# A hybrid decoder layer on one core: memory attention of two samples at a time, and three PSUM tiles of the recurrence in other banks

## The chip, the cores and the metric

The kernel runs on one core of one Trainium2 chip. The metric is device time in microseconds (us) of one execution, as a median over runs. Engines: PE does matmuls (PEld its weight loads), DVE, ACT and POOL do elementwise work, SP issues the weight DMAs and POOL's own queue (GpSimd) the rest.

## The reference

One decoder layer on 256 prompt tokens and 64 sample tokens (8 samples of 8), all in fp32:

```
xn = RMSNorm(x); p = xn @ w_in            # RWKV r,k,v,decay,a,gate | SWA q,k,v | memory q | 3 gates
A: RWKV-7, 12 heads of 64:  S = S*w + (S@-kk)(kk*a) + v k;  o = S @ r      # a scan over tokens
   o = (groupnorm(o) + bonus) * (sigmoid(gl) @ w_gate_up)
B: sliding-window attention (128), 12 query and 4 key heads, learned sinks
C: cross attention, 4 heads of 128, into 256 memory tokens per sequence:
   s = q . mk * 128**-0.5;  o = softmax(s) @ mv     # prompt: computed mk, mv; sample b: its cache_mem_k/v
merged = sum_i sigmoid(gate_i) * (o_i @ w_br_i);  h = x + RMSNorm(merged @ w_o)
y = h + RMSNorm((gelu(conv3(z_gate)) * z_val) @ w_ffn_down)
```

The change touches branch A (the recurrence) and the sample half of branch C.

## The kernel before, in words

Every weight matrix is streamed once in blocks of 128 x 128. A weight chunk `raw` comes by SP's queue, ACT casts its high half `wh` (L374, L97) and DVE takes the low half `wl` (L375, L98); `mm3` (L101 to L104) then does three matmuls of 320 columns per block. These "big" matmuls make up most of the program, and all other work of PE is put in between them.

What puts it there is `pump` (L404): the recurrence and the attention are generators, "threads", that issue some instructions and yield a number, the modelled time until their next piece may stand; between pieces `step` (L378) issues one block of big matmuls and moves a modelled clock on by 0.405. The order of PE's instructions is therefore written out when the program is built, and kept. For DVE, ACT, POOL and SP a scheduler sets the order.

The recurrence (about 90 to 530 us) goes over six pairs of heads, hp0 to hp5, in chunks of 32 tokens: 8 of the prompt, 2 of the samples. Each pair has three generators.
- `early` (L509) builds the operands `ar`, `bk` on DVE and ACT; PE takes the scores of all chunks into two PSUM tiles, `ps1` and `ps2` (L566, L571, L572); DVE masks them into `BT` (L569), POOL sends them through DRAM (L579, L581) to `NI`.
- `inverse` (L633) inverts the triangles of the chunks on DVE (L643 to L663), a long chain of multiplies and reductions; its result goes by DRAM (L666, POOL) and back as `IT` (four DMAs of L671, POOL).
- `late` (L677) solves (L693), takes the samples' states in (L714; ACT copies the result to `Wu`, L716), forms the chunk steps (L724 on PE into two banks; DVE adds them into `AB`, L727, and into `ar`, L730), starts the state in `psb` (L734), turns the 64 sample rows `Wu` by four small matmuls with the identity (L739, tile `psu`), which DVE adds to `AU` (L743, one instruction for each head), and starts the output `pso` from `BT` and `AU` (L749, 16 matmuls). Then the chain over chunks runs, PE (L753) and ACT by turns, each step with a yield of 1.2 (HOP). Behind it come the sample states (L769, L771 to L773), the group norm (L780, L781, L783; `rstd` with L130, POOL's power L136 and the copy L139; L147, L789), and the gate (L793, tile `psg`) with L794 and L795.

PSUM in the recurrence has eight banks: `big` two, `pea` two and `pch` two (both hand out tiles named `sm`; `bank()` in `late` takes one of `pch`), `pso` one and `psb` one. A tile of `pea` or `pch` is handed out again when the readers of the tile before last are done.

In the attention (about 530 to 800 us) PSUM is `big`, four banks of `smp` and two accumulators. `mem_sample` (L931) goes over the 8 samples: keys `ck` and values `cv` by POOL's queue (L937, L939, two buffers each), four score matmuls (L944), softmax (L885), two transposes (L902) and a DVE copy (L905), and eight matmuls into `po` (L952). The rows of a group of 32 that do not belong to the sample have probability 0 by the mask `smask`, so that four samples sum up in one tile.

Of the kernel before, what the change touches and what calls it, by code (L numbers as in the profile page):

```python
# [9 lines left out]
F32 = mybir.dt.float32  # L10
# [6 lines left out]
T = 320  # L17
TP = 256
# [21 lines left out]
SOFT = 3.5  # L40
SSOFT2, TRN2 = 9.0, 3.6
TRN = 2.0
# [21 lines left out]
def tile_hybrid_step(ctx: ExitStack, tc: tile.TileContext, i, o):  # L64
    nc = tc.nc
    V, A, G, PE = nc.vector, nc.scalar, nc.gpsimd, nc.tensor
# [9 lines left out]
    C = {n: cst[:, s] for n, s in COFF.items()}  # L76
# [351 lines left out]
    with tc.tile_pool(name="rws", bufs=1, side="right") as rws, tc.tile_pool(name="rwp", bufs=2, side="right") as rwp, \  # L428
# [80 lines left out]
        def early(hp):  # L509
# [58 lines left out]
            def masked(pv, lo, hi, mask):  # L568
                V.tensor_mul(out=BT[:, lo:hi, 64:128], in0=pv, in1=C[mask].unsqueeze(1).to_broadcast([128, hi - lo, 64]))  # L569

            ps1 = pea.tile([128, 512], F32, tag="sm", name="sm").rearrange("p (c t) -> p c t", t=64)  # L571
            ps2 = pea.tile([128, 512], F32, tag="sm", name="sm").rearrange("p (c t) -> p c t", t=64)  # L572
            scores(ps1, 0, 8)
            scores(ps2, 8, 10)
            masked(ps1, 0, 8, "tmask")
# [101 lines left out]
        def late(hp, ar, pc, bonus, BT, it, AU, AP):  # L677
# [9 lines left out]
            def bank():  # L687
                return pch.tile([128, 512], F32, tag="sm", name="sm")
# [43 lines left out]
            for c in range(8):  # L732
                for h in range(2):
                    PE.matmul(psb[fss[h], 64 * c:64 * c + 64], BT[fss[h], c, 0:64], AU[fss[h], c, 64:128],  # L734
                              start=c == 0, stop=c == 7, skip_group_check=True)
            psu = bank()
            for cc in range(2):
                for h in range(2):
                    PE.matmul(psu[uss[h], 64 * cc:64 * cc + 64], Wu[fss[h], 32 * cc:32 * cc + 32], C["ident"][fss[h], fss[h]], start=True, stop=True)  # L739
            SA = rw1.tile([128, 8, 64], F32, tag="SA", name="SA")  # L740
            A.activation(out=SA[:, 0, :], in_=psb[:, 0:64], func=AF.Copy, scale=pc[:, 0:1])
            for h in range(2):
                V.tensor_add(out=AU[uss[h], 8:10, 64:128], in0=psu[uss[h], 0:128].rearrange("p (c v) -> p c v", v=64), in1=AU[uss[h], 8:10, 64:128])  # L743
            UVm = rw1.tile([128, 512], F32, tag="UVm", name="UVm").rearrange("p (c s v) -> p c s v", s=4, v=64)
            G.tensor_mul(out=UVm, in0=AU[:, 8:10, 64:128].unsqueeze(2).to_broadcast([128, 2, 4, 64]),
                         in1=C["smask"].unsqueeze(1).unsqueeze(3).to_broadcast([128, 2, 4, 64]))
# [42 lines left out]
            V.tensor_mul(out=ob, in0=ob, in1=rn)  # L789
            A.activation(out=ob, in_=ob, func=AF.Identity, scale=col("lnw", hp), bias=col("lnb", hp))  # L790
            yield 2.0
            psg = pea.tile([128, 512], F32, tag="sm", name="sm")[:, :T]
            PE.matmul(psg, lw[:, 1, cs], lora[1], start=True, stop=True)  # L793
            V.tensor_add(out=ob, in0=ob, in1=bonus)  # L794
            V.tensor_mul(out=ob, in0=psg, in1=ob)  # L795
# [51 lines left out]
    with tc.tile_pool(name="at", bufs=1, side="right") as at, tc.tile_pool(name="at2", bufs=2, side="right") as at2, \  # L847
# [37 lines left out]
        def softmax(src, n, scale, th, keep=None):  # L885
            mx = at2.tile([128, 1], F32, tag="mx" + th, name="mx")
            V.tensor_reduce(out=mx, in_=src, axis=AX.X, op=ALU.max)
            V.tensor_scalar(out=mx, in0=mx, scalar1=-scale, scalar2=None, op0=ALU.mult)
            pr = at2.tile([128, 384], F32, tag="pr" + th, name="pr")[:, :n]
            sm = at2.tile([128, 1], F32, tag="sum" + th, name="sum")  # L890
            A.activation(out=pr, in_=src, func=AF.Exp, scale=scale, bias=mx, accum_out=sm)
            V.reciprocal(out=sm, in_=sm)
            if keep is None:
                V.tensor_scalar(out=pr, in0=pr, scalar1=sm, scalar2=None, op0=ALU.mult)
            else:
                V.tensor_scalar(out=pr, in0=pr, scalar1=sm, scalar2=keep, op0=ALU.mult, op1=ALU.mult)
            return pr
# [31 lines left out]
            state["om"] += 1  # L929

        def mem_sample():  # L931
            for b in range(8):
                bg, s = b // 4, b % 4
                if s == 0:
                    po = accp.tile([128, 512], F32, tag="accs", name="psos")
                ck = at2.tile([128, 4, 256], F32, tag="ck", name="ck")
                nc.gpsimd.dma_start(out=ck, in_=i["cmk"][b])  # L937
                cv = at2.tile([128, 2, 512], F32, tag="cv", name="cv")
                nc.gpsimd.dma_start(out=cv, in_=i["cmv"][b])  # L939
                yield 4.0  # L940
                pss = smp.tile([128, 512], F32, tag="sm", name="sm")
                qc = TP + 32 * bg
                for h in range(4):
                    PE.matmul(pss[32 * h:32 * h + 32, 0:256], MQ[:, h, qc:qc + 32], ck[:, h, :], start=True, stop=True,  # L944
                              tile_position=(0, 32 * h))
                pr = softmax(pss[:, 0:256], 256, MS, "s", C["smask"][:, s:s + 1])
                yield SOFT
                pt = transposed(pr, ((0, 128), (128, 128)), "s")
                yield TRN
                for kb in range(2):  # L950
                    for h in range(4):
                        PE.matmul(po[32 * h:32 * h + 32, 0:128], pt[:, 128 * kb + 32 * h:128 * kb + 32 * h + 32],  # L952
                                  cv[:, kb, 128 * h:128 * h + 128], start=s + kb == 0, stop=s + kb == 4, tile_position=(0, 32 * h))
                if s == 3:
                    ob = at2.tile([128, 128], F32, tag="ob", name="ob")
                    A.copy(out=ob, in_=po[:, 0:128])
                    yield TRN
                    pst = smp.tile([128, 512], F32, tag="sm", name="sm")
                    PE.transpose(pst[:, 0:128], ob, C["ident"])
                    split(OMH[:, :, qc:qc + 32], OML[:, :, qc:qc + 32], pst[:, 0:128].rearrange("p (h t) -> p h t", t=32))  # L960
            state["om"] += 1
# [440 lines left out]
```

## Time and profile before

| | |
|---|---|
| median of 3 runs | 2039.72 us (2036.27 to 2040.2) |
| the profiled execution | 2036.6 us, its span 2034.8 |
| PE busy, of the span | 1981.6 us (97%) |
| DVE, ACT, POOL busy | 1215.6 (60%), 829.2 (41%), 195.7 (10%) |
| mean granted TensorE clock | 0.988 |

A busy share is an average over stages. The rows below are taken from three kinds of view: busy time in stretches of the span, the list of what an engine waited for, and the timeline, in which a row is one instruction or a run of like ones ("x32"; a matmul of fp32 data is counted twice, since it runs in two passes), and in brackets the idle time of that engine just ahead and what ended it.

### The profile page before, as it was taken

The page shows a single profiled execution, that of the slowest core. Times are in us where ns is not written, and L with a number is a line of the kernel's source. Part 1 is how long each engine was busy: PE and PEld are TensorE (multiplying, and loading weights), DVE is VectorE, ACT ScalarE, POOL GpSimd, SP SyncE. Part 2 cuts the span into 40 slices and gives each one's busy share as a digit, 9 for nine tenths or more (in the row PEclk, how much of TensorE's full clock was granted, in tenths as well). Part 3 has the DMA queues.
Part 4 walks back from the last instruction along what each step waited for, and adds up shares of the span by engine and source line. Part 5 has one row for each costly group of instructions (what it writes and reads, how often), then busy time and mean ns, then how long its engine had stood idle before and what let it go on. Part 6 is the DMA issues. An engine that isn't in the chain of part 4 may idle for free.

```text
span 2034.8 us, 36379 instructions
## 1 busy us (share of the span) xinstructions
PE 1981.6 (97%) x14888; PEld 1928.4 (95%) x14888; DVE 1215.6 (60%) x2019; ACT 829.2 (41%) x1353; POOL 195.7 (10%) x446
## 2 busy tenths in 40 slices
PE   8999898899999999999999999999999999999997
PEld 8888898889998999999999999999999999999997
DVE  7788868874467754444447653554555555555456
ACT  5544344333444433333444433333343333343335
POOL 4412122211200000000100100000000000000001
PEclk9999899999999999999999999999999999999999
DMA  7543343333645444544552444454444444444433
GB/s 277 174 140 120 95 134 102 101 103 128 203 169 160 136 130 153 160 152 150 194 187 91 155 145 153 148 179 161 150 151 147 154 146 155 146 155 146 151 135 127
DMA packets 89688, 303.28 MB, mean 149 GB/s; under 512 B 11500, under 2 KB 13190, under 8 KB 89504
## 3 DMA queue, kind: packets, MB, share of 16 engines
q1 hardware_dynamic: 79920, 273.42, 40.1%
q0 software_dynamic: 8880, 26.71, 3.9%
q8 instruction: 117, 1.92, 0.4%
q10 hardware_dynamic: 720, 0.82, 0.1%
q14 instruction: 51, 0.42, 0.1%
HBM read 293.53 MB, written 9.34 MB: 149 GB/s over the span
## 4 chain that ended last, share of the span: by engine, by line
PE 57%; issue 5%; POOL 1%; DVE 0%; ACT 0%; POOLq 0%; DVEq 0%
PE bigps L102 18%; PE bigps L103 18%; PE bigps L104 18%; PE bigps L1171 0%; PE bigps L1169 0%; PE bigps L1172 0%; POOL merged L1094 0%; POOL yacc L1259 0%; POOL yacc L1260 0%; DVE MG L845 0%; PE sm L147 0%; POOL rsr L1119 0%; PE sm L1244 0%; PE sm L1112 0%; PE sm L1247 0%
## 5 line engine op out<-in xcount | busy, mean ns | idle before, releaser
L102 PE MATMUL bigps<-XH,wh 128*128 128x320 f32 x2656 | 843.7, 318 | 0.9 <-ACT gt L862 0.8
L104 PE MATMUL bigps<-XH,wl 128*128 128x320 f32 x2656 | 824.0, 310 | 1.4 <-DVE wl L375 1.3
L103 PE MATMUL bigps<-XL,wh 128*128 128x320 f32 x2656 | 823.7, 310 | 0.0
L98 DVE TENSOR_TENSOR wl<-raw,wh 128x1024 fp32r<-128x1024 f32 (+1 forms) x299 | 357.5, 1195 | 275.3 <-ACT wh L97 274.7
L97 ACT CAST wh<-raw 128x1024 fp32r<-128x1024 f32 (+1 forms) x299 | 306.5, 1025 | 521.5 <-PE bigps L103 412.8
L102 PEld LDWEIGHTS bigps<-XH,wh 128*128 128x128 f32 x2656 | 501.6, 189 | 14.1 <-issue 8.6
L103 PEld LDWEIGHTS bigps<-XL,wh 128*128 128x128 f32 x2656 | 501.9, 189 | 2.2 <-issue 0.2
L104 PEld LDWEIGHTS bigps<-XH,wl 128*128 128x128 f32 x2656 | 501.3, 189 | 2.4 <-DVE wl L375 2.4
L375 DVE TENSOR_TENSOR wl<-raw,wh 128x1024 fp32r<-128x1024 f32 (+2 forms) x212 | 243.2, 1151 | 184.5 <-ACT wh L374 182.0
L374 ACT CAST wh<-raw 128x1024 fp32r<-128x1024 f32 (+2 forms) x212 | 208.4, 984 | 313.0 <-PE bigps L103 250.9
L103 PE MATMUL bigps<-fl,wh 128*128 128x320 f32 x704 | 217.5, 309 | 0.0
L102 PE MATMUL bigps<-fh,wh 128*128 128x320 f32 x704 | 217.4, 309 | 0.0
L104 PE MATMUL bigps<-fh,wl 128*128 128x320 f32 x704 | 217.4, 309 | 0.0
L102 PEld LDWEIGHTS bigps<-fh,wh 128*128 128x128 f32 x704 | 132.2, 188 | 0.2 <-ACT fh L152 0.2
L103 PEld LDWEIGHTS bigps<-fl,wh 128*128 128x128 f32 x704 | 132.2, 188 | 0.1
L104 PEld LDWEIGHTS bigps<-fh,wl 128*128 128x128 f32 x704 | 132.2, 188 | 0.0
L1228 DVE TENSOR_TENSOR yacc<-yacc,bigps 128x320 f32<-128x320 f32 x80 | 38.9, 487 | 84.4 <-PE bigps L104 84.4
L1202 POOL COPY cout<-zp 128x9 f32<-128x9 f32 x88 | 15.5, 206 | 734.0 <-DVE zp L1199 734.0
L102 PE MATMUL bigps<-MG,wh 128*128 128x320 f32 x208 | 64.4, 309 | 0.3 <-ACT MG L844 0.3
L103 PE MATMUL bigps<-MG,wh 128*128 128x320 f32 x208 | 64.3, 309 | 0.0
L104 PE MATMUL bigps<-MG,wl 128*128 128x320 f32 x208 | 64.3, 309 | 0.0
L1198 DVE TENSOR_TENSOR zp<-bigps,S 128x256 f32<-128x256 f32 x44 | 18.7, 425 | 57.0 <-PE bigps L104 57.0
(407 smaller groups left out, 2358.4 us busy)
## 6 DMA issues: line engine op xcount, KB each, us to landing
raw<-in_wup SPq DMA_DIRECT2D x176, 512.0 KB, 3.5
raw<-in_win SPq DMA_DIRECT2D x164, 512.0 KB, 3.6
raw<-in_wdn SPq DMA_DIRECT2D x80, 512.0 KB, 3.2
raw<-in_wo SPq DMA_DIRECT2D x32, 512.0 KB, 3.7
raw<-in_wbr_rw SPq DMA_DIRECT2D x16, 384.0 KB, 3.2
raw<-in_wbr_sw SPq DMA_DIRECT2D x16, 384.0 KB, 3.1
ck<-in_cmk POOLq DMA_DIRECT2D x8, 512.0 KB, 5.1
cv<-in_cmv POOLq DMA_DIRECT2D x8, 512.0 KB, 4.2
```

What stands on the lines that cost most here:

```text
L97: A.copy(out=h, in_=raw)
L98: V.tensor_sub(out=l, in0=raw, in1=h.bitcast(F32))
L102: PE.matmul(ps, h, xh, start=start, stop=False)
L103: PE.matmul(ps, h, xl, start=False, stop=False)
L104: PE.matmul(ps, l, xh, start=False, stop=stop)
L374: A.copy(out=h, in_=c[2])
L375: V.tensor_sub(out=l, in0=c[2], in1=h.bitcast(F32))
L1198: V.tensor_mul(out=zp[:, 2:258], in0=psz[:, 0:TP], in1=S2[:, 0:TP])
L1202: G.tensor_copy(out=cout[:, j, :, e], in_=zp[:, 256 + e:337 + e:10])
L1228: V.tensor_add(out=yacc[:, m, :], in0=yacc[:, m, :], in1=ps)
```

## The change

1. The two score tiles of `early` come from `pch` instead of `pea`.
2. The gate's tile `psg` comes from `bank()`, so from `pch`, instead of `pea`.
3. `psu` is no bank of its own any more: it is columns 384 to 511 of the tile `pso`, which hold nothing else (the output has 0 to 255, the samples' rows 256 to 383). Its matmuls do not start the accumulation anew (`start=False`).
4. `mem_sample` takes two samples at a time: four DMAs ahead, eight score matmuls into one bank, two softmaxes, four transposes and one copy of 512 columns, sixteen matmuls; its yields are 5.0, 9.0 (SSOFT2) and 3.6 (TRN2) in place of 4.0, 3.5 (SOFT) and 2.0 (TRN).

```diff
--- before.py
+++ after.py
@@ -568,8 +568,8 @@
             def masked(pv, lo, hi, mask):
                 V.tensor_mul(out=BT[:, lo:hi, 64:128], in0=pv, in1=C[mask].unsqueeze(1).to_broadcast([128, hi - lo, 64]))
 
-            ps1 = pea.tile([128, 512], F32, tag="sm", name="sm").rearrange("p (c t) -> p c t", t=64)
-            ps2 = pea.tile([128, 512], F32, tag="sm", name="sm").rearrange("p (c t) -> p c t", t=64)
+            ps1 = pch.tile([128, 512], F32, tag="sm", name="sm").rearrange("p (c t) -> p c t", t=64)
+            ps2 = pch.tile([128, 512], F32, tag="sm", name="sm").rearrange("p (c t) -> p c t", t=64)
             scores(ps1, 0, 8)
             scores(ps2, 8, 10)
             masked(ps1, 0, 8, "tmask")
@@ -733,14 +733,15 @@
                 for h in range(2):
                     PE.matmul(psb[fss[h], 64 * c:64 * c + 64], BT[fss[h], c, 0:64], AU[fss[h], c, 64:128],
                               start=c == 0, stop=c == 7, skip_group_check=True)
-            psu = bank()
+            psu = pso[:, TP + 128:TP + 256]
             for cc in range(2):
                 for h in range(2):
-                    PE.matmul(psu[uss[h], 64 * cc:64 * cc + 64], Wu[fss[h], 32 * cc:32 * cc + 32], C["ident"][fss[h], fss[h]], start=True, stop=True)
+                    PE.matmul(psu[uss[h], 64 * cc:64 * cc + 64], Wu[fss[h], 32 * cc:32 * cc + 32], C["ident"][fss[h], fss[h]],
+                              start=False, stop=True, skip_group_check=True)
             SA = rw1.tile([128, 8, 64], F32, tag="SA", name="SA")
             A.activation(out=SA[:, 0, :], in_=psb[:, 0:64], func=AF.Copy, scale=pc[:, 0:1])
             for h in range(2):
-                V.tensor_add(out=AU[uss[h], 8:10, 64:128], in0=psu[uss[h], 0:128].rearrange("p (c v) -> p c v", v=64), in1=AU[uss[h], 8:10, 64:128])
+                V.tensor_add(out=AU[uss[h], 8:10, 64:128], in0=psu[uss[h], :].rearrange("p (c v) -> p c v", v=64), in1=AU[uss[h], 8:10, 64:128])
             UVm = rw1.tile([128, 512], F32, tag="UVm", name="UVm").rearrange("p (c s v) -> p c s v", s=4, v=64)
             G.tensor_mul(out=UVm, in0=AU[:, 8:10, 64:128].unsqueeze(2).to_broadcast([128, 2, 4, 64]),
                          in1=C["smask"].unsqueeze(1).unsqueeze(3).to_broadcast([128, 2, 4, 64]))
@@ -789,7 +790,7 @@
             V.tensor_mul(out=ob, in0=ob, in1=rn)
             A.activation(out=ob, in_=ob, func=AF.Identity, scale=col("lnw", hp), bias=col("lnb", hp))
             yield 2.0
-            psg = pea.tile([128, 512], F32, tag="sm", name="sm")[:, :T]
+            psg = bank()[:, :T]
             PE.matmul(psg, lw[:, 1, cs], lora[1], start=True, stop=True)
             V.tensor_add(out=ob, in0=ob, in1=bonus)
             V.tensor_mul(out=ob, in0=psg, in1=ob)
@@ -929,29 +930,40 @@
             state["om"] += 1
 
         def mem_sample():
-            for b in range(8):
-                bg, s = b // 4, b % 4
-                if s == 0:
+            for b2 in range(4):
+                bg, s0 = b2 // 2, 2 * (b2 % 2)
+                if s0 == 0:
                     po = accp.tile([128, 512], F32, tag="accs", name="psos")
-                ck = at2.tile([128, 4, 256], F32, tag="ck", name="ck")
-                nc.gpsimd.dma_start(out=ck, in_=i["cmk"][b])
-                cv = at2.tile([128, 2, 512], F32, tag="cv", name="cv")
-                nc.gpsimd.dma_start(out=cv, in_=i["cmv"][b])
-                yield 4.0
+                kv = []
+                for s in range(2):
+                    ck = at2.tile([128, 4, 256], F32, tag="ck", name="ck")
+                    nc.gpsimd.dma_start(out=ck, in_=i["cmk"][2 * b2 + s])
+                    cv = at2.tile([128, 2, 512], F32, tag="cv", name="cv")
+                    nc.gpsimd.dma_start(out=cv, in_=i["cmv"][2 * b2 + s])
+                    kv.append((ck, cv))
+                yield 5.0
                 pss = smp.tile([128, 512], F32, tag="sm", name="sm")
                 qc = TP + 32 * bg
                 for h in range(4):
-                    PE.matmul(pss[32 * h:32 * h + 32, 0:256], MQ[:, h, qc:qc + 32], ck[:, h, :], start=True, stop=True,
-                              tile_position=(0, 32 * h))
-                pr = softmax(pss[:, 0:256], 256, MS, "s", C["smask"][:, s:s + 1])
-                yield SOFT
-                pt = transposed(pr, ((0, 128), (128, 128)), "s")
-                yield TRN
-                for kb in range(2):
-                    for h in range(4):
-                        PE.matmul(po[32 * h:32 * h + 32, 0:128], pt[:, 128 * kb + 32 * h:128 * kb + 32 * h + 32],
-                                  cv[:, kb, 128 * h:128 * h + 128], start=s + kb == 0, stop=s + kb == 4, tile_position=(0, 32 * h))
-                if s == 3:
+                    for s in range(2):
+                        PE.matmul(pss[32 * h:32 * h + 32, 256 * s:256 * s + 256], MQ[:, h, qc:qc + 32], kv[s][0][:, h, :],
+                                  start=True, stop=True, tile_position=(0, 32 * h))
+                prs = [softmax(pss[:, 256 * s:256 * s + 256], 256, MS, "s", C["smask"][:, s0 + s:s0 + s + 1]) for s in range(2)]
+                yield SSOFT2
+                pst = smp.tile([128, 512], F32, tag="sm", name="sm")
+                for s in range(2):
+                    for kb in range(2):
+                        PE.transpose(pst[:, 256 * s + 128 * kb:256 * s + 128 * kb + 128], prs[s][:, 128 * kb:128 * kb + 128], C["ident"])
+                pt = at2.tile([128, 512], F32, tag="pt2", name="pt2", bufs=1)
+                V.tensor_copy(out=pt, in_=pst)
+                yield TRN2
+                for s in range(2):
+                    for kb in range(2):
+                        for h in range(4):
+                            c0 = 256 * s + 128 * kb + 32 * h
+                            PE.matmul(po[32 * h:32 * h + 32, 0:128], pt[:, c0:c0 + 32], kv[s][1][:, kb, 128 * h:128 * h + 128],
+                                      start=s0 + s + kb == 0, stop=s0 + s + kb == 4, tile_position=(0, 32 * h))
+                if s0 == 2:
                     ob = at2.tile([128, 128], F32, tag="ob", name="ob")
                     A.copy(out=ob, in_=po[:, 0:128])
                     yield TRN
```

Line numbers behind the first edit of `late` go up by one in the changed kernel (L743 is L744, L749 is L750, L753 is L754, and so on), and in `mem_sample` the scores L944 are L949. Three places show how the order moves.

PE, the recurrence, `late` of hp0, before (with the engines that each instruction waits for):
```order
L724 MATMUL sm<-BT,AU 64x96 [waits DVE_49,PE_49,Activation_49]
L724 MATMUL sm<-BT,AU 64x96 [waits DVE_49]
L724 MATMUL sm<-BT,AU 64x96 x6
L724 MATMUL sm<-BT,AU 64x96 [waits PE_49]
L724 MATMUL sm<-BT,AU 64x96 x5
L734 MATMUL psb<-AU,BT 64x64 x16
L739 MATMUL sm<-cst,Wu 32x64 [waits DVE_49,PE_49,Activation_49]
L739 MATMUL sm<-cst,Wu 32x64 x3
L749 MATMUL pso<-BT,AU 64x32 x16
```
And after:
```order
L724 MATMUL sm<-BT,AU 64x96 [waits DVE_49,PE_49,Activation_49]
L724 MATMUL sm<-BT,AU 64x96 [waits DVE_49]
L724 MATMUL sm<-BT,AU 64x96 x6
L724 MATMUL sm<-BT,AU 64x96 [waits PE_49]
L724 MATMUL sm<-BT,AU 64x96 x5
L734 MATMUL psb<-AU,BT 64x64 x16
L739 MATMUL pso<-cst,Wu 32x64 [waits Activation_49]
L739 MATMUL pso<-cst,Wu 32x64 x3
L750 MATMUL pso<-BT,AU 64x32 [waits DVE_49]
```
The order of PE is the same; L739 writes `pso`, loses its waits for DVE and PE and keeps ACT's, and the first L750 has a wait for DVE that L749 did not have.

On DVE nothing moves at this step: in every pair the two adds stand behind L727, L727, L730, L727, L727, L730, and read `pso` now.

POOL, where the late part of hp0 meets the inverse of hp1, before:
```order
L772 TENSOR_TENSOR S_1389<-S_1389,pc 128x512 [waits DVE_49]
L773 DMA out_wkvs<-S_1389 128x512 [waits DMASW2_49,Pool_49]
L666 DMA sc_2523<-R 120x192 [waits DMASW3_49,DVE_49]
L474 COPY shout<-pad 128x9 [waits Activation_49]
L681 DMA S_2208<-in_wkv 128x512 [waits DMASW4_49,DMASW2_49]
L469 MEMSET pad 128x1 [waits DVE_49,Pool_49]
L470 COPY pad<-shs 128x8
L671 DMA IT_775<-sc_2523 32x5x32 [waits DMASW5_49,DMASW3_49]
L671 DMA IT_775<-sc_2523 32x5x32 x2
L136 TENSOR_TENSOR rsr<-rsv,mhalf 128x6 [waits DVE_49]
L537 COPY pc<-rt 128x8 [waits Activation_49]
L538 COPY pc<-rt 128x8
```
And after:
```order
L774 DMA out_wkvs<-S_1389 128x512 [waits DMASW3_49,Pool_49]
L671 DMA IT_775<-sc_2522 32x5x32 [waits DMASW4_49,DMASW2_49]
L474 COPY shout<-pad 128x9 [waits Activation_49]
L671 DMA IT_775<-sc_2522 32x5x32 [waits DMASW5_49]
L681 DMA S_2207<-in_wkv 128x512 [waits DMASW3_49]
L469 MEMSET pad 128x1 [waits DVE_49,Pool_49]
L470 COPY pad<-shs 128x8
L671 DMA IT_775<-sc_2522 32x5x32
L671 DMA IT_775<-sc_2522 32x5x32 [waits DMASW0_49]
L537 COPY pc<-rt 128x8 [waits Activation_49]
L538 COPY pc<-rt 128x8
L136 TENSOR_TENSOR rsr<-rsv,mhalf 128x6 [waits DVE_49]
```
The group norm's power L136 stands behind all four `IT` loads and the two copies of `pc`, where it stood behind three loads; the load of the state S (L681) stands among the `IT` loads, and L666 ahead of the output of the states (L774, the L773 of before).

POOL, the begin of the attention, before:
```order
L937 DMA ck<-in_cmk 128x1024 [waits DMASW1_49,DMASW2_49,DMASW0_49,DMASW5_49,DVE_49,DMASW7_49,PE_49,Pool_49]
L939 DMA cv<-in_cmv 128x1024 [waits DMASW3_49]
L855 DMA amask<-in_amask 128x768 [waits DMASW4_49,DVE_49,PE_49]
L857 DMA snk<-in_sinks 128x16
L976 DMA out_vp<-Vt 128x256 [waits Activation_49]
L979 DMA out_vn<-Vn 64x256 [waits Activation_49]
L980 MEMSET QS 128x512
L937 DMA ck<-in_cmk 128x1024
```
And after:
```order
L940 DMA ck<-in_cmk 128x1024 [waits DMASW1_49,DMASW2_49,DMASW0_49,DMASW5_49,DVE_49,DMASW7_49,PE_49,Pool_49]
L942 DMA cv<-in_cmv 128x1024 [waits DMASW3_49]
L856 DMA amask<-in_amask 128x768 [waits DMASW4_49,DVE_49,PE_49]
L858 DMA snk<-in_sinks 128x16
L940 DMA ck<-in_cmk 128x1024
L942 DMA cv<-in_cmv 128x1024
```
The second sample's keys stand right behind the sinks, where three instructions lay between.

## Rows read from the trace of the kernel before

**Rows 1.** Busy time by stage: from:to, length, each engine's busy us, granted clock.
```profile
90.00:530.00 440.00, 409.74 (x3887) 383.78 (x3886) 323.46 (x569) 184.36 (x403) 87.57 (x149) 0.96 0.37 116
530.00:800.00 270.00, 268.34 (x2184) 250.83 (x2183) 164.53 (x408) 109.44 (x238) 19.46 (x35) 1.00 0.50 161
800.00:2034.80 1234.80, 1219.98 (x8319) 1217.90 (x8317) 658.30 (x946) 483.61 (x634) 50.59 (x209) 1.00 0.44 152
```
**Rows 2.** PE's waits: engine, tile, line, released by: us in total, times, longest.
```profile
PE sm L739 <- DVE ar L730: 17.6, 5, 4.6
PE sm L566 <- DVE ar L555: 3.2, 2, 1.8
PE sm L793 <- DVE rp L789: 2.2, 2, 1.9
```
**Rows 3.** PE's timeline, hp1: start us, us, instruction, [idle before, releaser].
```profile
245.08 0.64 PE L739 MATMUL sm<-cst,Wu 64*32 64x64 f32 x8 [4.04 <-DVE ar L730]
245.65 0.64 PE L749 MATMUL pso<-BT,AU 64*64 64x32 f32 x8
250.06 0.52 PE L753 MATMUL psb<-SA,AB 128*128 128x64 f32 x2
```
**Rows 4.** DVE's timeline, hp1.
```profile
244.64 0.29 DVE L730 TENSOR_TENSOR ar<-sm,ar 128x128 f32<-128x128 f32 x1
244.85 0.71 DVE L727 TENSOR_TENSOR AB<-sm,cst 64x192 f32<-64x192 f32 x2
245.77 0.57 DVE L743 TENSOR_TENSOR AU<-sm,AU 32x128 f32<-32x128 f32 x2
```
**Rows 5.** Busy time in three stretches behind waits of PE.
```profile
245.08:251.00 5.92, 5.92 (x53) 5.68 (x54) 5.57 (x10) 0.31 (x1) 1.04 (x1) 0.50 0.01 3
206.70:210.10 3.40, 3.40 (x13) 3.14 (x14) 3.40 (x8) 0.47 (x1) 2.27 (x2) 0.55 0.00 0
100.21:104.00 3.79, 3.79 (x57) 3.71 (x58) 3.48 (x5) 0.00 (x0) 1.15 (x2) 1.00 0.42 116
```
**Rows 6.** Timeline of PE and DVE, hp5.
```profile
502.33 1.12 PE L749 MATMUL pso<-BT,AU 64*64 64x32 f32 x32
503.66 0.59 DVE L743 TENSOR_TENSOR AU<-sm,AU 32x128 f32<-32x128 f32 x2
```
**Rows 7.** Timeline of PE and DVE, hp0.
```profile
172.01 0.41 PE L739 MATMUL sm<-cst,Wu 64*32 64x64 f32 x8 [0.92 <-DVE ar L730]
172.35 1.12 PE L749 MATMUL pso<-BT,AU 64*64 64x32 f32 x32
172.68 0.57 DVE L743 TENSOR_TENSOR AU<-sm,AU 32x128 f32<-32x128 f32 x2
194.54 0.48 DVE L781 SCALAR_TENSOR_TENSOR rp<-sm,rp 128x320 f32<-128x320 f32 x1
```
**Rows 8.** DVE's timeline, hp1, behind the chain.
```profile
265.61 0.49 DVE L781 SCALAR_TENSOR_TENSOR rp<-sm,rp 128x320 f32<-128x320 f32 x1 [2.23 <-PE sm L780]
```
**Rows 9.** POOL's timeline, late part of hp0.
```profile
197.84 1.73 POOL L671 DMA_DIRECT2D IT<-sc  x3 [0.36 <-issue]
199.59 1.36 POOL L136 TENSOR_TENSOR rsr<-rsv,mhalf 128x6 f32<-128x6 f32 x1
```
**Rows 10.** PE's timeline around the first sample's scores.
```profile
536.91 0.31 PE L104 MATMUL bigps<-XH,wl 128*128 128x320 f32 x1
537.15 0.64 PE L944 MATMUL sm<-ck,MQ 128*32 128x256 f32 x8
537.72 0.41 PE L102 MATMUL bigps<-XH,wh 128*128 128x320 f32 x1
537.97 0.30 PE L103 MATMUL bigps<-XL,wh 128*128 128x320 f32 x1
```
**Rows 11.** POOL's timeline ahead of them.
```profile
534.12 0.54 POOL L857 DMA_DIRECT2D snk<-in_sinks  x1
```
**Rows 12.** Tile of the sample keys: DMA landing.
```profile
DMA to landing us min/median/max: 3.4/5.1/8.1
```

## The prediction

> **What bounds the kernel now.** I read the busy time by stage first, then PE's list of waits, then the order of rows around the largest wait, then POOL's and the DMA rows where the change moves something. By stage [rows 1] PE is the bound everywhere: it is busy for 409.74 of 440 us in the recurrence (90 to 530 us), for 268.34 of 270 in the attention and for 1219.98 of 1234.8 in the rest, which the change does not touch. So only PE's idle time, and time in which its granted clock is halved, can be won or lost. Of the idle time in the recurrence one line of the waits holds most [rows 2]: L739, the four matmuls that turn the sample rows, stands 17.6 us for DVE L730. Five head pairs (hp) of six have that wait; hp0's is 0.92 [rows 7], so hp1 to hp4 have 16.7 together, about 4 each. In hp1 [rows 3] PE comes to L739 at about 241.04 and waits 4.04 us, until DVE, which is full of the next pair's inverse work, has done L730 (244.64 to 244.93 [rows 4]). Behind each such wait the granted clock is at 0.50, the lower of the two levels (1.2 GHz), for 5 to 6 us [rows 5]: PE does 5.92 us of work that the full clock does in half, so some 2.96 us go there too, in four such places, up to 12 in all.
>
> **The recurrence: the turned rows in the output's bank.** L739 now writes into `pso`, so it no longer needs a bank that L730 has read out, and its own wait is gone. But the tile is now one with what L749 (L750 after) writes, and L743 (L744), DVE's add of the turned rows, reads it in between. In the changed order L750 waits for DVE, and counted out on DVE's queue the post that it waits for is that of the second L744. L744 stands behind L727, L727, L730, L727, L727, L730, so the wait does not go: it moves one instruction down PE's queue and its end comes later on DVE's. Behind the waiting L750 stand its fifteen fellows, the big matmuls and the chain L754, so nothing of PE's passes it.
>
> In hp1 the two adds end at 245.77 + 0.57 = 246.34 [rows 4]; L739 started 0.15 behind L730's end, so L750 starts at about 246.48 where L749 started at 245.65 [rows 3]: +0.83. L739's own 0.57 us falls into the idle time ahead and is in that figure. hp2, hp3 and hp4 have the same instructions at nearly the same distances: 4 x 0.83 = +3.3. Does it add up over the pairs? PE's delay reaches DVE: L781 stands 2.23 us for PE's L780 in hp1 [rows 8], and there is a wait of DVE for PE in each of these four pairs. From there DVE's chain sets the next wait at L750, so a delay in one pair is not won back in the next. Bounds: 0.4 each where half is lost in such slack, 1.05 each were the release slower. I take 0.83.
>
> hp5 has a different order of DVE: a weight's cast stands between L730 and L743, which ends at 503.66 + 0.59 = 504.25 [rows 6], while L749 ran from 502.33 without waiting: 504.25 + 0.13 - 502.33 = +2.05, in a stretch that was full on PE, so all of it is lost. A halved clock may follow: behind the 1.9 us wait at L793 in hp0 the clock is 0.55 from 206.7 to 210.1, which costs about half of 3.4, 1.7; behind one of L566 of 1.8 there is none [rows 2, 5]. For each new wait of about 2 us I therefore take half of the dip, +0.85. Bounds +0.8 to +3.75.
>
> hp0 has the wait too: 172.68 + 0.57 + 0.13 - 172.35 = +1.03, but it costs nothing: DVE works without a gap up to L781, which starts at 194.54 with no idle time ahead of it [rows 7]. That work hides it; without the cover it is +1.03.
>
> By the Trainium skill ("PSUM — Partial Sum Buffer", Terms) TensorE and VectorE may not touch the same bank and quadrant of PSUM at once, and the compiler keeps them apart. The rows of before show the opposite case only: L743 from 172.68 inside L749's run from 172.35, with two banks [rows 7]. The rule speaks against the change even if the wait were not in the program: L744's 0.57 and L750 could no longer overlap, 0.57 for each of hp1 to hp5, +2.9, against my +5.35 for these five.
>
> **The recurrence: scores and gate in other banks.** PE's order is the same here; only waits for a free bank differ. The gate L793 stands 2.2 us for DVE L789 [rows 2], and that goes. But ahead of it the scheduler now puts POOL's L136 behind all four inverse loads L671, the state load L681 and the copies, where it stood right behind three of the loads [rows 9], and these loads wait for data to land. One load more (1.73 / 3 = 0.58), L681's issue, a DMA like these, and some small copies are about 1.7 in all (0.58 to 1.8). L139 waits for L136, so the spread of hp0's norm, and with it hp1's scores behind it on DVE, comes 1.7 later. Half of that is taken back where L793's wait stood, so +0.85, and for a dip behind it half of 1.7 again, +0.85. Bounds 0 to +3.4.
>
> **The attention.** The number of matmuls stays; 4 pairs instead of 8 samples make 4 groups of scores, 4 of transposes and 4 of products fewer. A group costs its edges: from the last big matmul to the group's first 0.24 us, and from the next big one to its successor 0.25 [rows 10], against a pitch of 1219.98 / 8319 = 0.147 [rows 1]. So 0.09 + 0.10, about 0.2 for each of 8 groups of scores and products; of a group of transposes I take half, 0.1 for 4: -2.0 us.
>
> Against it: the first pair's scores need the second sample's keys. POOL issues them now behind the first keys and values, the mask and the sinks, at 534.12 + 0.54 = 534.66 [rows 11]. Landing takes 3.4, 5.1 or 8.1 us (least, median, most) [rows 12]; at the median they are there at 539.8. L949 stands nine big matmuls further down than L944 did, at 537.15 + 9 x 0.147 = 538.5 [rows 10]: a wait of 1.3 (0 to 4.3), and with half a dip +0.85. The later pairs' loads have a whole pair's work to hide them; without that cover each costs what the first does. So the attention is -2.0 + 1.3 + 0.85 = +0.15 (bounds -2.0 to -2.0 + 4.3 + 1.7 = +4.0).
>
> By the Trainium skill ("DMA: Bandwidth & Descriptors", Anatomy of one DMA — SWDGE (gpsimd) path) a load issued from GpSimd takes 2.0 us and its bytes at 436 GB/s, 3.2 us for 512 KB; the keys would then be there at 537.9 and the wait and its dip gone, 2.15 us less in the sum. The trace's median of 5.1 is well above it, so I keep the row.
>
> **Sum.** +3.3 (hp1 to hp4) + 2.05 + 0.85 (hp5) + 0.85 + 0.85 (POOL in hp1) + 0.15 (attention) = +8.05 us on a profiled execution of 2036.6 us (span 2034.8 and 1.8 around it): 2044.65. The median of the runs shown is 2039.72, with a lowest of 2036.27; the middle of their spread, 2038.2, is 1.6 above the profiled execution, so the time to expect of runs is 2044.65 + 1.6, about 2046. All low bounds together give 1.6 + 0.8 + 0 - 2.0 = +0.4, all high ones 4.2 + 3.75 + 3.4 + 4.0 = +15.35.
>
> **Rivals.**
> *The wait goes after all* (faster). If L750 waited only for an early post of DVE, as L739 did not have to, PE would run on at 241.04 in hp1. Then the 16.7 us of hp1 to hp4 and the 12 of halved clock come back. Next is late L753: with L739, L749 and the big matmuls at full clock PE is there at about 243.8 (250.06 before [rows 3]), and AB's second half is done at 244.85 + 0.71 = 245.56 [rows 4], so about 1.8 is waited there in each, 7.2 in all. 2036.6 - 16.7 - 12 + 7.2 + 0.15 = about 2015. For it: L739's wait is the largest there is. Against it: L744 needs L739 and DVE reaches it in order, and the order after names the DVE wait at L750. That the change doesn't do what it says is this one's mirror: it does put the rows elsewhere, but the wait that it takes off L739 is back one row further down.
>
> *The delays vanish in slack* (no change). hp2 to hp4 begin with DVE's chain, and if the idle time of DVE there takes the +0.83 each, only hp5's 2.05 is left, against -2.0 + 1.3: 2036.6 + 1.35, about 2038, in runs 2038 to 2041. For it: DVE has idle time in every pair, as before L781 [rows 8]. Against it: that idle time is itself spent waiting for PE.
>
> *The keys come late and the clock falls* (slower still). The second keys come right behind the first keys and values and beside SP's stream of weights; at 8.1 us they land at 542.8, a wait of 4.3 and a full dip of 1.7 to 3 (2.35). With full dips at hp5 and at hp1's scores: 3.3 + 3.75 + (0.85 + 1.7) + 4.3 + 2.35 - 2.0 = +14.25, about 2051, in runs 2052. It decides from a landing of over 6 us.
>
> **Chances.** My forecast 0.58, the keys late 0.12, no change 0.18, the wait gone 0.12. Two runs' sets of this kernel can't be told apart within about 0.2%, 4 us. The forecast's own range is 2041 to 2051; of its 0.58 some 0.43 lie over 2043.8, slower by 0.2%, and 0.15 within. With the late keys slower is 0.55; with 0.17 of the no-change case within 0.2% is 0.32; its last 0.01 and the wait gone make faster 0.13. The range of 2035 to 2053 leaves out the case in which the wait goes and the ends.
>
> **What would show it.** Right: PE's waits after list L750 for DVE's AU L744 with about 24 us in six places (17.6, some 0.9 more in each of five, since L739's own time and L744 are now part of it, and hp5's 2), and none at L739; the halved clock stands behind it as before; L949 waits for a DMA of keys once, by 1 to 2 us; L793's wait is gone. Wrong: no DVE wait at L750, or one of less than 17 us; full clock in hp1 to hp4; a recurrence that ends before its old end of about 530 us; an attention stage that is over 3 us shorter.

## The result, and the profile after

The changed kernel takes 2050.61 us (2050.33 to 2053.05, 3 runs) against 2039.72: 10.9 us slower by the medians; ratio 1.0062, 95% interval 1.0046 to 1.0078. Its profiled execution has a span of 2048.6 us, 13.8 more than that of before, which was near the low end of its own runs.

PE's waits, in the form of [rows 2]:

```profile
PE pso L750 <- DVE AU L744: 24.7, 6, 5.7
PE sm L566 <- DVE ar L555: 4.2, 3, 1.8
PE sm L566 <- DVE rp L796: 4.1, 2, 2.4
PE sm L949 <- DMA ck<-in_cmk: 2.5, 1, 2.5
PE sm L130 <- ACT rp L784: 1.4, 1, 1.4
...
PE sm L794 <- DVE BT L569: 0.8, 1, 0.8
```

L739's 17.6 us are gone and L750 has 24.7 in six places; L793's 2.2 for L789 is gone, and L566 waits more. PE's timeline in hp1 and hp5, which answers to [rows 3, 6]:

```profile
245.30 0.41 PE L739 MATMUL pso<-cst,Wu 64*32 64x64 f32 x8
250.82 1.92 PE L750 MATMUL pso<-BT,AU 64*64 64x32 f32 x32 [5.10 <-DVE AU L744]
255.23 0.52 PE L754 MATMUL psb<-SA,AB 128*128 128x64 f32 x2
...
511.39 0.41 PE L739 MATMUL pso<-cst,Wu 64*32 64x64 f32 x8
513.67 1.92 PE L750 MATMUL pso<-BT,AU 64*64 64x32 f32 x32 [1.87 <-DVE AU L744]
518.09 0.52 PE L754 MATMUL psb<-SA,AB 128*128 128x64 f32 x2
```

And DVE's in hp1 and hp5 [rows 4, 6]:

```profile
250.19 0.57 DVE L744 TENSOR_TENSOR AU<-pso,AU 32x128 f32<-32x128 f32 x2
...
511.74 0.26 DVE L730 TENSOR_TENSOR ar<-sm,ar 128x96 f32<-128x96 f32 x1
511.91 1.22 DVE L375 TENSOR_TENSOR wl<-raw,wh 128x1024 fp32r<-128x1024 f32 x1
513.05 0.57 DVE L744 TENSOR_TENSOR AU<-pso,AU 32x128 f32<-32x128 f32 x2
```

L739 runs as soon as PE reaches it, and L750 stands until the second add is done (250.19 + 0.57 = 250.76). In hp5 the add itself stands behind a weight's cast. Stretches behind the six waits (length, PE, PEld, DVE, ACT, POOL busy, granted clock, DMA share, GB/s), as in [rows 5]:

```profile
174.03:182.00 7.97, 7.97 (x91) 7.04 (x92) 7.16 (x11) 1.50 (x3) 1.66 (x1) 0.58 0.01 2
250.82:257.00 6.18, 6.18 (x49) 6.12 (x50) 5.97 (x7) 0.84 (x2) 1.04 (x1) 0.50 0.01 3
318.38:325.00 6.62, 6.62 (x51) 6.22 (x51) 5.66 (x8) 1.59 (x3) 1.59 (x1) 0.50 0.01 2
387.09:393.00 5.91, 5.91 (x48) 5.84 (x49) 5.28 (x6) 1.36 (x2) 1.04 (x1) 0.50 0.00 0
457.79:462.00 4.21, 4.21 (x41) 4.15 (x42) 3.29 (x5) 1.39 (x2) 1.90 (x1) 0.50 0.00 0
513.67:520.00 6.33, 6.33 (x49) 6.26 (x50) 0.00 (x0) 0.31 (x1) 1.05 (x1) 0.50 0.28 85
```

PE is busy through all of them, at half the clock (in hp0 at 0.58, since the stretch there begins at full clock). hp0 and hp5 had no such stretch in the profile of before. Against before, the sixteen matmuls (L749, now L750) start later by 1.68, 5.17, 6.26, 8.13, 9.57 and 11.34 us in hp0 to hp5, and hp5's gate (L793, now L794) by 14.19. The attention behind it gives 0.6 of that back.

### The profile page after: what moved, and what is told of

It is laid out like the page before. It is cut to its first block, busy times and chain, and to the rows that moved or that the text cites. A ratio compares the mean times of both kernels' runs of the same rounds, so it can differ in the third digit from the quotient of the medians.

```text
span 2048.6 us, 36350 instructions
## 1 busy us (share of the span) xinstructions
PE 1986.8 (97%) x14888; PEld 1936.8 (95%) x14888; DVE 1212.3 (59%) x2015; ACT 828.6 (40%) x1353; POOL 197.3 (10%) x446
## 4 chain that ended last, share of the span: by engine, by line
PE 62%; issue 11%; POOL 1%; DMA 1%; DVE 0%; ACT 0%; POOLq 0%; ACTq 0%
PE bigps L102 19%; PE bigps L103 19%; PE bigps L104 19%; PE bigps L1183 0%; PE bigps L1181 0%; PE bigps L1184 0%; PE sm L903 0%; DMA ck<-in_cmk 0%; PE sm L1026 0%; DMA merged<-in_xT 0%; PE sm L949 0%; POOL yacc L1271 0%; PE psos L964 0%; PE pso L922 0%; PE pso L1037 0%
```

## The experiments

Theory W is the prediction's: the wait moves to L750 and grows, and the halved clock behind it costs as well. Rival B: the banks of the scores and gate, with POOL's new order, cost the time. Rival K: the second sample's keys do. Each kernel was timed in rounds with the kernel before, but for one that was timed once (hp5 alone, e10), which has no ratio. Two lengths from each profile separate the places: the recurrence, from the first scores L566 to hp5's gate, and the attention, from that gate to the first big matmul on branch B's output (OSH).

| kernel | ratio to before (95%) | recurrence us | attention us |
|---|---|---|---|
| before | 1 | 430.0 | 287.05 |
| changed | 1.0062 (1.0046 to 1.0078) | 444.1 | 286.4 |
| own bank for the rows (e1) | 1.0016 (1.0007 to 1.0026) | 433.9 | 288.3 |
| rows in pso only (e2) | 1.0057 (1.0042 to 1.0072) | 444.4 | 287.0 |
| pairs only (e3) | 1.0014 (1.0004 to 1.0024) | 433.0 | 289.8 |
| changed, rows last (e4) | 0.9960 (0.9947 to 0.9974) | 421.7 | 288.4 |
| scores and gate only (e5) | 1.0009 (0.9999 to 1.0019) | 432.3 | 287.1 |
| pairs, keys first, longer pause (e6) | 1.0024 (1.0014 to 1.0033) | 431.0 | 292.3 |
| before, rows last (e7) | 0.9932 (0.9916 to 0.9948) | 420.3 | 287.05 |
| e7, chain 4.0, with e6's pairs (e8) | 0.9939 (0.9919 to 0.9959) | 416.9 | 288.0 |
| changed, filler (e9) | 1.0153 (1.0138 to 1.0169) | 459.9 | 288.0 |
| e7, chain 2.8 (e11) | 0.9972 (0.9962 to 0.9982) | 424.6 | 287.2 |
| e11 with pairs, keys first (e12) | 0.9959 (0.9944 to 0.9974) | 426.7 | 285.0 |

The recurrence of before is built unchanged in e3 and e6 too, and took 430.0, 433.0 and 431.0 us: in e3 and e6 the clock halves in hp0 as well. Differences of up to 3 us in that column say nothing.

**The third edit undone.**
```diff
-            psu = pso[:, TP + 128:TP + 256]
+            psu = bank()
```


> The changed kernel with its third edit undone: the turned rows L739 go to a bank of their own again (pch), scores, gate and the pairs of samples stay changed. Theory W (the wait moved to L750 and the halved clock behind it cost the time): most of the +10.9 us goes, 2040 to 2044 us; L739 waits 17 to 19 us for L730 as before, L750 for nothing, and hp0 and hp5 have no stretch of halved clock at this place. Rival B (the banks of the scores and POOL's order cost it, L136 behind all loads): 2047 to 2051 us, the loss of about 4 us up to hp1's L724 is still there. Rival K (the keys): 2048 to 2051, the recurrence ends about where it did after the change.

Ratio 1.0016, 2043.42 us. L739 has its wait back (18.1 us in five places), none is left at L750, hp0 and hp5 run at full clock there. The recurrence is 10.2 us shorter than in the changed kernel. Theory W; some 3 us stay with the other edits.

**The third edit alone**, on the kernel before.
```diff
-            psu = bank()
+            psu = pso[:, TP + 128:TP + 256]
```


> The kernel before with the third edit alone: L739 writes into pso. Theory W: slower by 8 to 12 us, 2048 to 2052; L750 waits about 24 us in six places and L739 for nothing; the recurrence's L793 of hp5 comes 10 to 14 us later than before. Rival B: within 3 us of before, since POOL's order is what costs. Rival K: within 3 us of before.

Ratio 1.0057, 2051.19 us: alone it costs as much as the whole change. L750 waits 25.2 us in six places, and with no other edit in the program the recurrence takes 444.4 us. Rival K falls, and of rival B the banks fall. POOL's new order does not fall by this run: L136 stands behind all four L671 here too, and in the order of before in e1, e3 and e5. So it comes with the third edit, not with the banks, to which the prediction gave it. It is one delay of 1.6 us in hp0 (below), so it is not what makes L750 wait in six places.

**The pairs alone.**
```diff
-            for b in range(8):
+            for b2 in range(4):
...
```


> The kernel before with the pairs of samples alone. Theory W: within 2 us of before (2.0 won at the groups' edges, 1 to 2.5 lost at the first wait for keys). Rival K (the keys cost): slower by 5 us or more. A third view, that pairs win a lot which the rest hides: faster by 4 us or more.

Ratio 1.0014, between the expectations and close to "no change". The scores stand 3.0 us for the second keys, and the clock is halved from 544 to 550 us, so the attention takes 2.7 us more. In the changed kernel the same wait has no such stretch behind it, and the attention takes 0.6 us less:

```profile
552.67 0.62 PE L949 MATMUL sm<-ck,MQ 128*32 128x256 f32 x2
555.79 1.09 PE L949 MATMUL sm<-ck,MQ 128*32 128x256 f32 x14 [2.50 <-DMA ck<-in_cmk]
```

**The rows behind the sixteen matmuls**, in the changed kernel: same tile, same adds, the other order on PE.
```diff
+            for c in range(8):
+                for h in range(2):
+                    PE.matmul(pso[fss[h], 32 * c:32 * c + 32], AU[fss[h], c, 64:128], BT[fss[h], c, 64:96],
             psu = pso[:, TP + 128:TP + 256]
...
-            for c in range(8):
-                for h in range(2):
-                    PE.matmul(pso[fss[h], 32 * c:32 * c + 32], AU[fss[h], c, 64:128], BT[fss[h], c, 64:96],
...
             yield HOP
```


> The changed kernel with the sixteen matmuls L749 put ahead of the four L739 (same tile pso, same adds), so no matmul of PE stands behind DVE's read of pso until much later. Theory W: L750's wait of 24.7 us is gone; what is late next is the chain's first matmul, which needs DVE's AB (L727): 1.5 to 2.5 us in each of hp1 to hp4; with half of the halved clock gone 2018 to 2031 us, faster than both kernels. Rival B and K: the wait merely moves to the chain with its whole length, 2045 to 2051 us.

2030.4 us, ratio 0.9960: faster than both. L750's wait is gone, and the chain waits 4.8 us for AB (three places) and 3.4 for ACT's copies (two). So what the prediction's rival "the wait goes after all" described does happen, once none of the sixteen matmuls stands behind DVE's read.

**Scores and gate alone.**
```diff
-            ps1 = pea.tile(
+            ps1 = pch.tile(
...
-            psg = pea.tile(
+            psg = bank()[:, :T]
```


> The kernel before with the first two edits alone: scores and gate in pch. Theory W: within 3 us of before (the run without the third edit was 1.0016 and the pairs alone 1.0014, so nearly nothing is left for these two): L793's wait of 2.2 us is gone, and hp1's scores L566 wait 1 to 2.4 us instead. Rival B: slower by 5 us or more.

Ratio 1.0009, interval 0.9999 to 1.0019: no change that can be told. L793's 1.95 and the halved clock behind it are gone, and the second part of hp2's scores (L566 at 214 us) waits 2.39 instead of 0.62, with a halved clock behind that. The recorded texts call these scores hp1's; hp1's own ran at about 152 us. POOL's order is that of before here, and the wait is the same as in the changed kernel; POOL's order is not its cause.

**Pairs with both keys first and a pause of 9.0 before the scores.**
```diff
+                for s in range(2):
+                    cv = at2.tile([128, 2, 512], F32, tag="cv", name="cv")
...
-                yield 5.0
+                yield 9.0
```


> The kernel before with the pairs of samples, the keys of both samples loaded ahead of the values, and a pause of 9.0 instead of 5.0 before the scores. If the wait of 2.5 to 3.0 us for the second keys and the halved clock behind it are what the pairs cost, they go and the pairs' 2 us show: 2036 to 2041 us, no wait of the scores for a DMA, full clock from 540 to 552 us. If the pairs cost something else: the 1.0014 of the pairs alone stays, 2042 to 2045.

Slower, 1.0024, for a reason that neither side named. The wait for keys is gone and branch C's matmuls are reached 0.9 us earlier, but the longer pause puts the last pair's products (L965) right ahead of branch C's first matmuls (OMH), and PE waits at both and once more behind:

```profile
658.37 1.08 PE L965 MATMUL psos<-cv,pt 128*32 128x128 f32 x32 [1.89 <-DVE pt L959]
660.95 0.64 PE L102 MATMUL bigps<-OMH,wh 128*128 128x320 f32 x1 [0.79 <-ACT OMH L152]
...
679.53 0.42 PE L102 MATMUL bigps<-XH,wh 128*128 128x320 f32 x1 [1.77 <-ACT gt L862]
```

**The rows last, on the kernel before.**
```diff
-            psu = bank()
...
             for c in range(8):
                 for h in range(2):
                     PE.matmul(pso[fss[h], 32 * c:32 * c + 32], AU[fss[h], c, 64:128], BT[fss[h], c, 64:96],
...
+            psu = pso[:, TP + 128:TP + 256]
```


> The kernel before with the turned rows in pso and behind L749, nothing else changed. Theory W: the whole gain of that order without the other edits, 2025 to 2031 us, L739's wait of 17.6 gone and 5 to 8 us of it back at the chain's first matmuls. If the gain of the run with rows last came from the other edits with it (banks, pairs): 2035 to 2040.

2027.25 us, ratio 0.9932: the lowest median of all (e8 is not told apart from it), some 14 us under before by the medians and 8.9 by the two profiles. PE's waits, and the place in hp1:

```profile
PE psb L754 <- ACT SA L756: 6.5, 2, 3.3
PE psb L754 <- DVE AB L727: 4.1, 3, 1.7
```
```profile
241.67 1.07 PE L738 MATMUL pso<-BT,AU 64*64 64x32 f32 x32
242.67 0.41 PE L743 MATMUL pso<-cst,Wu 64*32 64x64 f32 x8
...
245.67 0.41 PE L754 MATMUL psb<-SA,AB 128*128 128x64 f32 x2 [1.07 <-DVE AB L727]
```

PE goes on at 243 where it stood until 245.08 [rows 3]; the chain's first matmul waits for AB by 1.1 to 1.7 us, as the prediction's rival had it, and ACT's copies are late twice. PE is at full clock from 241 to 254 us. With the edits of banks and pairs the same order gave 0.9960, so nothing shows that they help here.

**The chain later**, with e6's pairs.
```diff
-            yield HOP
+            yield 4.0
             for c in range(1, 8):
```


> The run before this one, with the keys-first pairs of the run before that, and a pause of 4.0 instead of 1.2 between L749 with the rows and the chain, so that seven more blocks of big matmuls stand there (about 3 us at full clock). Theory W: the waits of 1.4 to 1.8 us for AB in hp1 to hp3 go, and with them the halved clock behind: 2015 to 2025 us. Rival: the chain's later start only moves the loss to hp's end (the next pair's late part starts later, DVE's inverse waits for it), 2027 to 2035.

2029.0 us, not told apart from e7 and within the rival's range, though by another path than the rival's. The recurrence is shorter (416.9), AB is waited for nowhere, but ACT's copies are late:

```profile
PE psb L754 <- ACT SA L756: 12.9, 4, 5.3
```

In hp2, ACT's queue holds an early activation of a later pair (L531) ahead of the copy, and ACT is idle 5.46 us before it, for DVE. The longer attention takes 0.9 back.

**Filler in the wait.** Small matmuls of zeros ahead of L739.
```diff
+            for _ in range((9, 21, 24, 24, 16, 6)[hp]):
+                PE.matmul(psu, zero, zero, start=False, stop=False, skip_group_check=True)
```


> The changed kernel with small matmuls of zeros (128 x 128, into the columns of pso that L739 then fills; they add nothing) put ahead of L739: 9, 21, 24, 24, 16 and 6 of them in hp0 to hp5, meant to be a little shorter than the waits at L750 (2.4, 5.1, 5.7, 5.6, 4.1, 1.9 us). PE is busy instead of idle and the wait's end is DVE's as before, so only the clock can change. If the halved clock behind L750 is the price of the idle time before it: L750's waits are together under 8 us, the clock stays full behind L750 in most pairs, and the time falls by 6 to 14 us, to 2037 to 2045. If the clock falls for another reason (the small matmuls, the chain behind): 2049 to 2056, the clock halved as before.

2071.7 us, and the question stays open: the wait did not stay where it was. L754 (its L750) waits 25.2 us although PE comes up to 5.6 us later, because the scheduler moved the add behind nine more instructions of the inverse. DVE in hp2:

```profile
321.94 0.26 DVE L732 TENSOR_TENSOR ar<-sm,ar 128x96 f32<-128x96 f32 x1
322.11 0.80 DVE L656 TENSOR_TENSOR prod<-R,NI 120x384 f32<-120x384 f32 x1
...
327.83 0.75 DVE L658 TENSOR_REDUCE W<-prod 120x24 f32<-120x576 f32 x1
328.50 0.57 DVE L748 TENSOR_TENSOR AU<-pso,AU 32x128 f32<-32x128 f32 x2
```

Here DVE's place for the add sets the wait's end, not PE's time of arrival. On the clock it has one pair: hp0 waits 2.40 us as in the changed kernel (2.37), with the filler ahead, and the clock stays at 1.00 until 182; there it fell to 0.50. (In hp5 it stays at 1.00 too, but the wait is 0.68 there, for 1.87.) One pair is a hint and no proof.

**hp5 alone with the rows last**, in the changed kernel, timed once.
```diff
+            if hp == 5:
+                for c in range(8):
...
             psu = pso[:, TP + 128:TP + 256]
```


> The changed kernel with the rows behind the sixteen matmuls in the last pair (hp5) alone. Hp5's own price is its wait of 1.87 and the halved clock behind, together 4.8 us between L739 and L770. Theory W: no wait at hp5, full clock from 512 to 520 us, hp5's gate comes 4 to 5 us earlier against its L724 than in the changed kernel, the other five pairs as there. Rival: the wait goes to the chain, L754, and the gate comes as late as before.

From L724 to the gate hp5 takes 30.47 us (542.92 - 512.45), against 35.42 in the changed kernel (544.43 - 509.01) and 30.63 before: 4.95 less, at full clock from 512 to 520. So hp5's price is its own. The span is no shorter (2048.7): hp5's L724 is reached 3.44 us later than in the changed kernel (the halved stretches of hp0 to hp2 are longer in this run), and the attention takes 288.1 us, 1.65 more, with a halved clock from 554 to 558.

**A pause of 2.8 ahead of the chain**, on e7.
```diff
-            yield HOP
+            yield 2.8
             for c in range(1, 8):
```


> The kernel before with the rows in pso behind L749 and a pause of 2.8 instead of 1.2 ahead of the chain (four more blocks of big matmuls, 1.8 us). The waits for AB of 1.4 to 1.8 go as they did with a pause of 4.0. Theory W: 2021 to 2026 us. If the chain's waits for ACT's copies (12.9 us with 4.0) set the time: 2025 to 2030, no better than with 1.2.

2034.24 us, ratio 0.9972: slower than 1.2. AB's wait is gone, ACT's copies cost 8.7 us, and L566 and L794 wait more for DVE (L794 3.0 for its L547). That is the second view's side, but the time lies above its range too: those waits for DVE were in neither sum.

**The same with the pairs, keys first, the pause before the scores as it was.**
```diff
-                yield 9.0
+                yield 5.0
```


> The run before this one with the pairs, keys first and the old pause of 5.0 before the scores. If the pairs' 2 us are to be had when the second keys come in time and the products aren't late: 2 us or so under the run before this one, the time from hp5's gate to the first use of the SWA branch 284 to 286.5 us in place of 287.05. If not: the same or 1 to 5 us more, with a new wait named in the list.

2032.36 us, which isn't told apart from the run before it; the attention takes 285.0 us, 2.2 less than there, with a wait of 1.6 left for keys. The four other kernels whose attention is that of before (e2, e5, e7, e11) took 287.0 to 287.2, so in the profile the pairs' 2 us exist; coming late with the keys or with the products spends them. The medians do not show them clear of noise.

## Why the prediction was right

The direction and the mechanism were right, and the time is in the range; the sum came out low.

*The wait.* It was to move to L750 with about 24 us in six places; it has 24.7. That it would not go was the step on which the sign hung, and e1, e2, e4 and e7 show that it is the cause.

*hp1 to hp4.* +0.83 each was the difference of two waits' ends. From L724 to L750 the changed kernel loses 0.85, 0.80 and 0.91 in hp1 to hp3; in hp4 it loses nothing (9.88 behind at L724, 9.57 at L750). The halved clock adds 1.05 in hp2 and 0.5 in hp3, which was costed at nothing. Another 1.26 is lost between hp3's chain and hp4's L724, where the clock is halved from 434 to 439 us with no wait of PE ahead of it; the profile of before has no such stretch, and its cause is open. From 4.32 at hp1's L724 to 9.40 at hp5's it is +5.1, where +3.3 stood in the sum.

*hp0.* Costed at nothing, hidden by DVE's work: this term failed. The wait of 2.37 has a halved clock behind it to 182 us, so the chain's end is 4.76 late, more than DVE's slack: L782 (L781 before the change) waits 1.10 for PE and is 2.01 late. From hp0's L724 to hp1's the delay against before grows by 4.10 us (0.22 to 4.32), and in e2, with the rows alone, by 3.25. So most of it comes with the rows: hp0's wait, and POOL's part below.

*POOL's order.* The delay was there, by another edit than forecast: it goes with the rows in `pso` (e2). DVE's L139 waits for L136 in the changed kernel, e2 and e5 (banks only) by

```profile
204.75 0.36 DVE L139 COPY rex<-rsr 128x384 f32<-128x384 f32 x1 [3.55 <-POOL rsr L136]
206.07 0.36 DVE L139 COPY rex<-rsr 128x384 f32<-128x384 f32 x1 [3.54 <-POOL rsr L136]
202.83 0.36 DVE L139 COPY rex<-rsr 128x384 f32<-128x384 f32 x1 [1.97 <-POOL rsr L136]
```

and by 1.97 before. In the changed kernel DVE is 2.16 late at L134, which L136 reads, and 3.77 at L139 (204.75 for 200.98): 1.61 lost between the two, about the 1.7 forecast. The banks move PE's wait from L793 (1.95 before) to the second part of hp2's scores; the prediction counted only the gain:

```profile
216.03 0.51 PE L566 MATMUL sm<-ar,bk 64*64 64x64 f32 x8 [2.39 <-DVE rp L796]
```

So the +1.7 of the sum stood for a delay that came, but from another edit than the one it was put down to, which is luck; hp0's own delay came on top of it.

*hp5.* +2.05 measured as +1.94 at L750; the halved clock behind, taken at half of 1.7, cost 2.85 (2.91 in e2). The whole is 4.79 against before, and 4.95 against e10, where 2.9 stood.

*The attention.* +0.15 forecast; -0.6 in the profile of the changed kernel, -0.6 to +2.7 over the kernels with these pairs. The wait for keys was 2.5 to 3.0, for 1.3: landing has a median of 5.3 us here, but the second keys, issued at 548.85, ended PE's wait at 555.79, 6.9 later. The estimate of 3.2 us from the Trainium skill ("DMA: Bandwidth & Descriptors", Anatomy of one DMA — SWDGE (gpsimd) path), by which there would be no wait, is not what these runs show.

*The rivals.* "The wait goes after all" needed an order in which the read stands behind the matmuls; with it (e7) it came to -14 us by the medians and -8.9 by the profiles, not -21: the AB waits were smaller than in its sum (4.1 for 7.2), the clock gave back 8 of the 12, and the waits for ACT's copies (6.5) were not in it. The clock's part is PE's busy time by the share of the clock that it lacked, summed over 90 to 600 us: 14.6 us before, 23.9 after the change, 6.5 in e7. "The keys come late" named a landing of over 6 us as its sign, and that came, but with a wait of 2.5 for 4.3 and full clock behind it. It also had a full dip at hp5, which came. Its 2052 is nearer to the 2050.6 measured than the forecast's 2046, but the keys are not why: the attention got no longer.

*The size.* +8 was forecast against +10.9 of the medians and +13.8 of the profiles. In the profiles hp0 with POOL and the scores is 4.3 for 1.7, hp1 to hp4 5.1 for 3.3, hp5 4.8 for 2.9, the attention -0.6 for +0.15. The missing part is mostly halved clock, which was costed at nothing or at half: 3.1 behind hp0's wait before DVE's slack, 2.85 behind hp5's, 1.5 in hp2 and hp3.

## What to carry to other kernels

Putting a small result into a bank that a longer run of matmuls writes next saves a bank, but makes those matmuls wait for the reader; write the small result last, and that wait goes (e2 and e7 differ only in that order: 1.0057 and 0.9932; what is left at the chain is 10.6 us for 25.2). When a wait of TensorE falls away or grows, cost the granted clock behind it too: here it was the larger part. From 90 to 530 us PE's idle time was 30.3 us before, 37.1 after the change and 27.4 in e7, and the clock's part 14.6, 23.9 and 6.5. A longer pause in a written-out order also moves what the scheduler puts on the other engines, so read their queues again before costing it.

## What was not expected of the hardware

The clock after the same wait of the same program part differs from run to run: behind the unchanged L739 of hp0 it stays full in the profile of before (a wait of 0.92) and is halved for 3 to 7 us in e3 and e6 (waits of 1.11 and 1.35). The changed kernel's wait of 2.50 for keys was followed by full clock, e3's of 3.0 by 6 us at half. Why it falls behind one such wait and not behind another was not settled.
